# A state-space layer inside a trunk kernel: decay by two heads, exponent on ScalarE, skip and far parts added early

## The chip, the cores and the metric

The kernel runs on one core of a Trainium2 chip. A core has five engines that each run their own instructions in order and wait for one another by semaphores: TensorE (PE: matrix products and transposes; PEld is its weight load), VectorE (DVE), ScalarE (ACT), GpSimd (POOL) and SyncE (SP), which here only issues DMA transfers. Data lies in SBUF; TensorE writes into PSUM. The metric is the time of one execution on the device in microseconds. Before the change it is 2331.98 us, the median of 3 runs (2331.76 to 2332.18).

## What is computed

Two layers with 256 tokens of width 2048: layer 0 mixes tokens by attention (MLA), layer 1 by a Mamba-2 state-space mixer, and each is followed by an MLP with squared ReLU (2048 to 8192 to 2048). The change touches the state-space mixer and, by the size of a DMA ring, the two MLPs. The mixer, cut to what matters (64 heads of 64 in 8 groups, state 128, one chunk of 256 tokens, so the state starts at zero and the second term of y is zero):

```python
zxbcdt = h @ w_in
z, xbc, dt = split(zxbcdt)
xbc = silu(causal_depthwise_conv(xbc, conv_w, conv_b))
xs, b_in, c_in = split(xbc)                    # xs: 8 groups x 8 heads x 64
dt = softplus(dt + dt_bias)
a = -exp(a_log)
# ssd_chunked_scan
x_c = xs * dt
cum = cumsum(dt * a)
decay = exp(where(tril, cum[l] - cum[s], -inf))
cb = einsum('blgn,bsgn->blsg', c, b)
y = einsum('blsgh,bsghp->blghp', cb[..., None] * decay, x_c)
# after the scan
y = y + d_skip * xs
y = y * silu(z)
y = y * rsqrt(mean(y * y over the group's 512) + 1e-6)
return (y * norm_g) @ w_out
```

## The kernel before

**Products in three parts.** Every weight piece (128 x 1024, float32, `wraw`, loaded by SyncE at L88) is split into a high half `wh`, rounded by ScalarE (L103), and a low half `wl`, the rest, by VectorE (L104). A product of float32 is then three products: high by high (L324), low of the activations by high of the weights (L325), high by low of the weights (L328). The MLPs use the same with a scheme of seven products (L595 to L597), in which some weight pieces are summed by VectorE and some by a GpSimd DMA that adds into SBUF as it lands (L200, `wrx`). A flow object loads six pieces ahead and converts three ahead.

**Order.** TensorE runs in the order in which the program is written. The order of the other engines is set by the tile scheduler from its own estimates, and buffers come from pools of fixed numbers.

**Stages.** Attention runs from 0 to about 262 us of the profiled execution, the first MLP to about 945, the state-space mixer from about 960 to 1668, the second MLP to 2330.

**The state-space mixer runs by ticks.** A block of weight products is a list of keys; one key is 24 matmuls, after which `tick()` runs what `later(n, fn)` has put off by n ticks, and then `pump()`. `SSM_ORDER` names the blocks: x0 to x7 (the x of a group, with its convolution), z0 to z7 (its gate), and o0 to o3 (the output projection). A `z` block of group g is named two steps or so after its `x`, so while x of group g + 2 is brought in, the gate of group g is finished.

- *x of a group* (`x_block`, L1159 on): after the convolution TensorE transposes x into PSUM (L1173), ScalarE copies it to SBUF as two halves `xtm` (L1175), GpSimd multiplies the first half by `edge` (L1183), and one tick later TensorE forms the part of the second 128 tokens that comes from the first 128 (`far`, L1187), which VectorE scales into `far` (L1189).
- *a head* (L1203 on): SyncE broadcasts one row of `cumD`, the cumulated log decay, to 128 partitions (`cm`, L1207). VectorE adds the negative of the own row's value and takes the minimum with 0 (L1211, twice), ScalarE takes the exponent (L1212), VectorE multiplies by dt and by the scores `cb` (L1214, twice). A tick later TensorE multiplies by x (L1223).
- *the end of a group*, in the eighth head's product: GpSimd multiplies x by the skip gain `dg` (L1227, twice) and adds `far` to the second half (L1229), VectorE adds half of that to y from PSUM (L1230, twice).
- *the gate* (`z_block`): GpSimd multiplies by the gate (L1255, twice), ScalarE sums squares (L295), then VectorE L288, GpSimd L289 (a power of −0.5), VectorE L1259 and L1261 (twice), and one tick later TensorE transposes the result (L309) for the output projection, which ScalarE and VectorE evacuate as two halves (L298, L299).

Small helpers that record instructions for many callers have one line each: L103, L104, L288, L289, L295, L309, L376 (gain tiles), L419 (the residual sum).

## Time and profile before

| what | value |
|---|---|
| median of the runs | 2331.98 us |
| the profiled execution | 2332.54 us, span 2330.6 us |
| TensorE busy | 2313.0 us, 99% of the span, granted clock 1.00 |
| VectorE busy | 1907.8 us, 82% |
| ScalarE busy | 1384.4 us, 59% |
| GpSimd busy | 193.2 us, 8% |
| DMA | 510.74 MB, mean 219 GB/s |

A line number is a line of the kernel, and a row of a group or of the timeline reads: line, engine, operation, the tile written, an arrow, the tiles read, the shape, the number of instructions; then busy time and the mean of one, or in the timeline first the start and the duration. Text in square brackets or behind a bar is idle time of that engine just before, and the instruction that ended it. A timeline row with x2 or x8 is a run of that many equal instructions.

### The profile page before, as it was taken

What the parts mean: (1) busy time and instruction counts of PE and PEld (TensorE: products, weight loads), DVE (VectorE), ACT (ScalarE), POOL (GpSimd) and SP (SyncE); (2) the same over time, 40 slices, a digit from 0 to 9 for tenths busy, and PEclk for the clock granted to TensorE, in tenths of its full rate; (3) what the DMA queues carried; (4) which work ended last, traced back from release to release, by engine and by line L of the source; (5) the groups of instructions that cost most, each with busy time, mean ns of one, the idle gap of its engine ahead of it and who ended that gap; (6) DMA issues with size and microseconds to landing.
All of it is one profiled execution on the core that took longest, in us unless ns stands there. A gap on an engine that the chain in (4) does not pass through costs nothing. (4 is left out here: it accounts for less than half of the span.)

```text
span 2330.6 us, 30315 instructions
## 1 busy us (share of the span) xinstructions
PE 2313.0 (99%) x10799; PEld 1924.8 (83%) x10799; DVE 1907.8 (82%) x2469; ACT 1384.4 (59%) x1869; POOL 193.2 (8%) x209
## 2 busy tenths in 40 slices
PE   9999999999999999999999999999999999999999
PEld 7788888888888888888888888888888888888887
DVE  7776697998899897677788768666888899989885
ACT  6665566666566656555555455445566656666663
POOL 1331000000000000000022101110000000000000
PEclk9999999999999999999999999999999999999999
DMA  8434678878877877665566666656687888788874
GB/s 310 142 114 142 195 232 254 242 249 255 263 240 247 265 214 247 203 197 180 170 195 201 204 188 194 198 175 201 206 254 231 254 264 239 250 265 246 249 228 164
DMA packets 152151, 510.74 MB, mean 219 GB/s; under 512 B 17152, under 2 KB 26304, under 8 KB 152000
## 3 DMA queue, kind: packets, MB, share of 16 engines
q1 hardware_dynamic: 143712, 479.37, 62.9%
q0 software_dynamic: 8064, 29.36, 7.7%
q8 instruction: 85, 1.39, 0.2%
q14 instruction: 66, 0.54, 0.1%
q10 hardware_dynamic: 224, 0.07, 0.0%
HBM read 506.58 MB, written 2.16 MB: 218 GB/s over the span
## 5 line engine op out<-in xcount | busy, mean ns | idle before, releaser
L103 ACT ACTIVATE wh<-wraw 128x1024 fp32r<-128x1024 f32 (+2 forms) x818 | 859.8, 1054 | 635.2 <-PE acc L325 287.7
L104 DVE TENSOR_TENSOR wl<-wraw,wh 128x1024 fp32r<-128x1024 f32 (+2 forms) x818 | 991.9, 1224 | 250.2 <-ACT wh L103 239.6
L595 PE MATMUL yp<-wh,k 128*128 128x512 f32 x896 | 349.8, 390 | 0.0
L596 PE MATMUL yp<-wl,k 128*128 128x512 f32 x896 | 348.9, 389 | 0.4 <-DVE wl L104 0.3
L597 PE MATMUL yp<-wh,k 128*128 128x512 f32 x896 | 348.8, 389 | 0.0
L324 PE MATMUL acc<-wh,xt 128*128 128x512 f32 x704 | 280.4, 398 | 2.6 <-ACT wh L103 2.6
L325 PE MATMUL acc<-wh,xt 128*128 128x512 f32 x704 | 274.7, 390 | 0.0
L103 ACT ACTIVATE wh<-wrx 128x1024 fp32r<-128x1024 f32 x168 | 178.0, 1060 | 136.9 <-PE yp L597 105.3
L104 DVE TENSOR_TENSOR wl<-wrx,wh 128x1024 fp32r<-128x1024 f32 x168 | 203.8, 1219 | 37.4 <-ACT wh L103 37.4
L596 PEld LDWEIGHTS yp<-wl,k 128*128 128x128 f32 x896 | 168.2, 188 | 35.8 <-DVE wl L104 1.3
L597 PEld LDWEIGHTS yp<-wh,k 128*128 128x128 f32 x896 | 168.2, 188 | 35.0
L595 PEld LDWEIGHTS yp<-wh,k 128*128 128x128 f32 x896 | 168.2, 188 | 34.6
L324 PE MATMUL acc<-wh,k 128*128 128x512 f32 x496 | 196.8, 397 | 0.0
L325 PE MATMUL acc<-wh,k 128*128 128x512 f32 x496 | 193.3, 390 | 0.0
L328 PE MATMUL acc<-wl,xt 128*128 128x512 f32 x704 | 188.6, 390 | 0.0
L595 PE MATMUL st<-wh,xt 128*128 128x512 f32 x448 | 176.8, 395 | 0.0
L596 PE MATMUL st<-wl,xt 128*128 128x512 f32 x448 | 174.8, 390 | 0.0
L597 PE MATMUL st<-wh,xt 128*128 128x512 f32 x448 | 174.8, 390 | 0.0
L324 PEld LDWEIGHTS acc<-wh,xt 128*128 128x128 f32 x704 | 132.6, 188 | 30.7 <-ACT wh L103 4.6
L328 PEld LDWEIGHTS acc<-wl,xt 128*128 128x128 f32 x704 | 132.2, 188 | 28.2
L325 PEld LDWEIGHTS acc<-wh,xt 128*128 128x128 f32 x704 | 132.5, 188 | 25.8
L200 POOL DMA_DIRECT2D wrx<-mi x56 | 48.9, 874 | 1140.3 <-DVE wl L104 1034.4
(291 smaller groups left out, 3475.7 us busy)
## 6 DMA issues: line engine op xcount, KB each, us to landing
wraw<-mi SPq DMA_DIRECT2D x256, 512.0 KB, 5.2
wraw<-mo SPq DMA_DIRECT2D x256, 512.0 KB, 5.3
wraw<-si SPq DMA_DIRECT2D x160, 512.0 KB, 4.0
wraw<-so SPq DMA_DIRECT2D x64, 512.0 KB, 4.3
wrx<-mi SPq DMA_DIRECT2D x56, 512.0 KB, 5.2
wrx<-mi POOLq DMA_DIRECT2D x56, 512.0 KB, 8.0
wraw<-wo SPq DMA_DIRECT2D x32, 512.0 KB, 3.6
wraw<-ukv SPq DMA_DIRECT2D x16, 512.0 KB, 5.0
```

What stands on the lines that cost most here:

```text
L103: self.last = nc.scalar.activation(h[:, v], raw[:, v], AF.Copy)
L104: nc.vector.tensor_tensor(lo[:, v], raw[:, v], h[:, v].bitcast(F32), ALU.subtract)
L200: nc.gpsimd.dma_start(st["b11"].tile, quarter(d, 1, 0), accum_op=ALU.add)
L324: nc.tensor.matmul(accs[t][:, :n], ah, wh[:, q, :], start=first and kt + q == 0, stop=False)
L325: nc.tensor.matmul(accs[t][:, :n], al, wh[:, q, :], start=False, stop=False)
L328: nc.tensor.matmul(accs[t][:, :n], lhs(kt + q, t)[0], wl[:, q, :], start=False, stop=en and q == nk - 1)
L595: nc.tensor.matmul(b, ah, wh, start=first and q == 0, stop=False)
L596: nc.tensor.matmul(b, ah, wl, start=False, stop=False)
L597: nc.tensor.matmul(b, al, wh, start=False, stop=last and q == 1)
```

## The change

It has these parts, all in the state-space mixer but the last:

1. Heads are worked by two. One broadcast of 512 values brings the cumulated decay of two heads (`cm`, four buffers as before but twice as wide). `cumT` holds the own values with their sign; ScalarE takes max(0, own − other) by an activation with a bias (L1214, four of 128 wide), and the exponent of its negative in one of 512 (L1215). VectorE then does one product of 512 wide by the scores (L1218).
2. dt is taken out of that product: VectorE makes a copy xd = x · dt from SBUF when x has been evacuated (L1180, twice a group), and the products read `xd`.
3. The skip gain is multiplied into x by GpSimd right after the `edge` product (L1187, twice, in place), and `far` is added by GpSimd as soon as it is there (L1194). At the group's end only VectorE's sum with y is left (L1231).
4. A group counts as ready for its gate one tick later.
5. The y banks are allocated by the helper, the backlog at which a head is taken each tick goes from 4 heads to 2 pairs, and below it a pair is taken every other tick.
6. The ring of descriptors for DMAs issued by GpSimd is set to 4096 bytes.

```diff
-            cm = sp.tile([P, S], F32, tag="cm", name=f"cm{h}", bufs=4)
-            nc.sync.dma_start(cm, cumD[h:h + 1].to_broadcast([P, S]))
-            m = sp.tile([P, 256], F32, tag="mt", name=f"mt{h}", bufs=6)
-            for t in range(2):
-                nc.vector.tensor_scalar(half(t), cm[:, t * P:(t + 1) * P], ncum[:, t, h:h + 1], 0.0, ALU.add, ALU.min)
-            nc.scalar.activation(m, m, AF.Exp)
-            for t in range(2):
-                nc.vector.scalar_tensor_tensor(half(t), half(t), dt[:, t, h:h + 1], cb[g][:, 256 * t:256 * t + P],
-                                               ALU.mult, ALU.mult)
+            m = sp.tile([P, 2, 2, P], F32, tag="cm", name=f"cm{h}", bufs=4)
+            nc.sync.dma_start(m.rearrange("p a t n -> p (a t n)"), cumD[h // 2:h // 2 + 1].to_broadcast([P, 2 * S]))
+            for k in range(2):
+                for t in range(2):
+                    nc.scalar.activation(m[:, k, t], m[:, k, t], AF.Relu, bias=cumT[:, t, h + k:h + k + 1], scale=-1.0)
+            nc.scalar.activation(m, m, AF.Exp, scale=-1.0)
+            v = m.rearrange("p a t n -> p a (t n)")
+            scores = cb[g][:, 0:2].rearrange("p t n -> p (t n)").unsqueeze(1).to_broadcast([P, 2, 2 * P])
+            nc.vector.tensor_tensor(v, v, scores, ALU.mult)
...
                     nc.scalar.activation(x, b, AF.Copy)
                     xg[g].append(x)
-                for i in range(8):
-                    hq.append((g, i, dg))
+                    w = sp.tile([P, 512], F32, tag="xd", name=f"xd{g}_{t}", bufs=4)
+                    nc.vector.tensor_tensor(heads_of(w), heads_of(x), spread(dt[:, t]), ALU.mult)
+                    xd[g].append(w)
+                for i in range(0, 8, 2):
+                    hq.append((g, i))
                 xw = self.scratch()
                 nc.gpsimd.tensor_tensor(heads_of(xw), heads_of(xg[g][0]), spread(edge[:, 0]), ALU.mult)
+                for t in range(2):
+                    nc.gpsimd.tensor_tensor(xg[g][t], xg[g][t], dg, ALU.mult)
 
                 def across():
...
-                    far[g] = sp.tile([P, 512], F32, tag="far", name=f"far{g}", bufs=2)
-                    nc.vector.tensor_tensor(heads_of(far[g]), heads_of(b), spread(edge[:, 1]), ALU.mult)
+                    far = self.scratch()
+                    nc.vector.tensor_tensor(heads_of(far), heads_of(b), spread(edge[:, 1]), ALU.mult)
+                    nc.gpsimd.tensor_tensor(xg[g][1], xg[g][1], far, ALU.add)
...
         def pump():
-            for _ in range(2 if len(hq) > HEAD_BACKLOG else 1):
-                if hq:
-                    g, i, dg = hq.pop(0)
-                    head(g, i, dg)
-                    if i == 7:
-                        break
+            turns[0] += 1
+            if hq and (len(hq) > HEAD_BACKLOG or turns[0] % 2):
+                heads(*hq.pop(0))
...
-                if i == 7:
+                if i == 6:
                     for t in range(2):
                         x = xg[g][t]
-                        nc.gpsimd.tensor_tensor(x, x, dg, ALU.mult)
-                        if t:
-                            nc.gpsimd.tensor_tensor(x, x, far[g], ALU.add)
                         nc.vector.scalar_tensor_tensor(x, x, 0.5, y[t], ALU.mult, ALU.add)
-                    ready.add(g)
+                    self.later(0, lambda: ready.add(g))
...
-HEAD_BACKLOG = 4
+HEAD_BACKLOG = 2
...
-    nc = bacc.Bacc("TRN2", target_bir_lowering=False, num_devices=1)
+    nc = bacc.Bacc("TRN2", target_bir_lowering=False, num_devices=1, dynamic_dma_scratch_size=4096)
```

The edits in the source also change the order that the scheduler gives to the engines. Three places follow.

GpSimd where x of group 5 is brought in, before (`xtm5_0` is the first half of group 5's x, `xtm3_0` and the `st` rows belong to the gate of group 3, `xtm4_0` to the gate of group 4; line, operation, tile written, tiles read, shape):

```order
L1255 TENSOR_TENSOR xtm3_0_11162<-s2_899_12348,xtm3_0_11162 128x512
L1255 TENSOR_TENSOR xtm3_1_11169<-s2_900_12351,xtm3_1_11169 128x512
L1183 TENSOR_TENSOR s2_908_12446<-xtm5_0_12435,edge_8774 128x512
L289 TENSOR_TENSOR st_912_12455<-st_911_12454,mhalf_91 128x2
L1255 TENSOR_TENSOR xtm4_0_11651<-s2_931_12821,xtm4_0_11651 128x512
L1255 TENSOR_TENSOR xtm4_1_11658<-s2_932_12824,xtm4_1_11658 128x512
L1227 TENSOR_TENSOR xtm5_0_12435<-xtm5_0_12435,gb_907_12444 128x512
L1227 TENSOR_TENSOR xtm5_1_12442<-xtm5_1_12442,gb_907_12444 128x512
L1229 TENSOR_TENSOR xtm5_1_12442<-xtm5_1_12442,far5_12582 128x512
```

And after the change:

```order
L1256 TENSOR_TENSOR xtm3_0_11089<-s2_914_12208,xtm3_0_11089 128x512
L1256 TENSOR_TENSOR xtm3_1_11098<-s2_915_12211,xtm3_1_11098 128x512
L1185 TENSOR_TENSOR s2_923_12310<-xtm5_0_12297,edge_8774 128x512
L1187 TENSOR_TENSOR xtm5_0_12297<-xtm5_0_12297,gb_920_12290 128x512
L1187 TENSOR_TENSOR xtm5_1_12306<-xtm5_1_12306,gb_920_12290 128x512
L289 TENSOR_TENSOR st_927_12321<-st_926_12320,mhalf_91 128x2
L1194 TENSOR_TENSOR xtm5_1_12306<-xtm5_1_12306,s2_932_12432 128x512
```

The two skip products of group 5 moved from behind two gates to a place ahead of L289, the power that belongs to the gate of group 3.

VectorE where x of group 4 is brought in, before (`mt37` is head 37's decay, `x00` the residual stream, `wl525` a weight piece's low half; the `st` and `s2` rows are the gate of group 2):

```order
L1214 SCALAR_TENSOR_TENSOR mt37_11864<-mt37_11864,dt_8772,cb4_10170 128x128 x2
L419 TENSOR_TENSOR x00_133<-acc_863_11565,x00_133 128x512
L419 TENSOR_TENSOR x10_137<-acc_864_11566,x10_137 128x512
L104 TENSOR_TENSOR wl525_11701<-wraw525_11585,wh525_11700 128x1024
L288 TENSOR_SCALAR st_871_11670<-st_858_11556 128x2
L1259 TENSOR_TENSOR st_873_11674<-st_872_11671,rs0_141 128x2
L1261 SCALAR_TENSOR_TENSOR s2_859_11557<-xtm2_0_10650,st_873_11674,gb_857_11554 128x512
L1261 SCALAR_TENSOR_TENSOR s2_860_11560<-xtm2_1_10657,st_873_11674,gb_857_11554 128x512
```

And after the change:

```order
L1218 TENSOR_TENSOR cm38_11821<-cm38_11821,cb4_10168 128x512
L419 TENSOR_TENSOR x00_133<-acc_875_11454,x00_133 128x512
L419 TENSOR_TENSOR x10_137<-acc_876_11455,x10_137 128x512
L1180 TENSOR_TENSOR xd4_0_11543<-xtm4_0_11541,dt_8772 128x512
L1180 TENSOR_TENSOR xd4_1_11552<-xtm4_1_11550,dt_8772 128x512
L104 TENSOR_TENSOR wl525_11587<-wraw525_11474,wh525_11586 128x1024
L288 TENSOR_SCALAR st_883_11564<-st_870_11445 128x2
L1260 TENSOR_TENSOR st_885_11568<-st_884_11565,rs0_141 128x2
L1262 SCALAR_TENSOR_TENSOR s2_871_11446<-xtm2_0_10615,st_885_11568,gb_869_11443 128x512
L1262 SCALAR_TENSOR_TENSOR s2_872_11449<-xtm2_1_10624,st_885_11568,gb_869_11443 128x512
```

The two x · dt products stand between the residual sums and L104, and with L104 ahead of the gate's L288.

ScalarE where x of group 3 is brought in, before (`mt26` and `mt27` are heads, `wh508` and `wh509` high halves of weight pieces, the two L295 the square sums of the gate of group 1):

```order
L1212 ACTIVATE mt26_11266<-mt26_11266 128x256
L103 ACTIVATE wh508_11141<-wraw508_11075 128x1024
L1212 ACTIVATE mt27_11274<-mt27_11274 128x256
L103 ACTIVATE wh509_11209<-wraw509_11093 128x1024
L1175 ACTIVATE xtm3_0_11162<-sm_833_11157 128x512
L1175 ACTIVATE xtm3_1_11169<-sm_834_11164 128x512
L295 ACTIVATE s2_837_11178,st_826_11064<-xtm1_0_10364,rs0_141 128x512
L295 ACTIVATE s2_838_11181,st_826_11064<-xtm1_1_10371,rs0_141 128x512
```

And after the change:

```order
L103 ACTIVATE wh508_11066<-wraw508_11004 128x1024
L1214 ACTIVATE cm30_11399<-cm30_11399,cumT_8773 128x128 x4
L1215 ACTIVATE cm30_11399<-cm30_11399 128x512
L103 ACTIVATE wh509_11130<-wraw509_11022 128x1024
L1177 ACTIVATE xtm3_0_11089<-sm_843_11084 128x512
L1177 ACTIVATE xtm3_1_11098<-sm_844_11093 128x512
L295 ACTIVATE s2_846_11107,st_835_10993<-xtm1_0_10349,rs0_141 128x512
L295 ACTIVATE s2_847_11110,st_835_10993<-xtm1_1_10358,rs0_141 128x512
```

The pair of heads 30 and 31, four activations and one exponent, stands ahead of a weight piece and of the evacuation of x.

## The prediction

> **What bounds the kernel now.** First the page: the span and the engines' busy time. The profiled execution took 2332.54 us, 0.56 above the median of the runs (2331.98), with a span of 2330.6.

> ```profile
> span 2330.6 us, 30315 instructions
> PE 2313.0 (99%) x10799; PEld 1924.8 (83%) x10799; DVE 1907.8 (82%) x2469; ACT 1384.4 (59%) x1869; POOL 193.2 (8%) x209
> ```

> TensorE sets the time, and the change adds and removes no matmul. So I looked at the stretch it edits, the state-space stage: one window of 480 us (columns: us, then busy us of PE, PEld, DVE, ACT, POOL, granted clock, DMA share, GB/s), and all that TensorE waits for between 1000 and 1600.

> ```profile
> 1120.00:1600.00 480.00, 478.94 (x2311) 398.23 (x2310) 356.21 (x595) 248.88 (x347) 78.67 (x56) 1.00 0.62 192
> PE sm L1065 <- ACT xtm L1175: 0.5, 1, 0.5
> PE sm L309 <- DVE s L1261: 0.3, 2, 0.2
> ```

> TensorE is idle 480.00 − 478.94 = 1.06 us there, at full clock. That is nearly all the change could win: work taken from VectorE or ScalarE is time TensorE does not wait for. What it can lose has no such cap, so the question is which results that TensorE needs come later.

> **Work that moves off the path.** Groups by line and shape, 1000 to 1600 (count | busy us, mean ns | idle before and its releaser):

> ```profile
> L104 DVE TENSOR_TENSOR wl<-wraw,wh 128x1024 fp32r<-128x1024 f32 x196 | 245.4, 1256 | 106.9 <-ACT wh L103 105.7
> L1214 DVE SCALAR_TENSOR_TENSOR mt<-mt,dt,cb 128x128 f32<-128x128 f32 x128 | 39.4, 349 | 2.6 <-ACT mt L1212 2.3
> L1211 DVE TENSOR_SCALAR mt<-cm,ncum 128x128 f32<-128x128 f32 x128 | 37.7, 338 | 0.0
> L1230 DVE SCALAR_TENSOR_TENSOR xtm<-xtm,y 128x512 f32<-128x512 f32 x16 | 10.9, 684 | 19.6 <-POOL xtm L1229 15.0 <-POOL xtm L1227 4.7
> L103 ACT ACTIVATE wh<-wraw 128x1024 fp32r<-128x1024 f32 x195 | 206.5, 1060 | 216.2 <-PE acc L325 175.8 <-issue 21.3 <-DVE mt L1211 6.9
> L1212 ACT ACTIVATE mt<-mt 128x256 f32<-128x256 f32 x64 | 25.4, 410 | 38.8 <-DVE mt L1211 38.6
> L1155 ACT ACTIVATE cb<-sm 128x128 f32<-128x128 f32 x6 | 1.6, 274 | 3.9 <-DVE cb L1154 3.3 <-PE y L1223 0.6
> L1175 ACT ACTIVATE xtm<-sm 128x512 f32<-128x512 f32 x16 | 8.7, 591 | 1.0 <-PE sm L1173 1.0
> L1229 POOL TENSOR_TENSOR xtm<-xtm,far 128x512 f32<-128x512 f32 x8 | 10.3, 1287 | 0.6
> ```

> VectorE loses L1211 and L1214, 77.1 us, and gains 32 products of 512 wide and 16 x·dt: at L1230's 0.684 each, 32.8. ScalarE loses 64 exponents (25.4 − their merger: 32 of 512 wide at L1175's 0.591 = 18.9) and gains 128 Relu at L1155's 0.274 = 35.1: net +28.6 over some 540 us. I cost all this at nothing: ScalarE was busy 248.9 of 480 us, and its main work, L103, stands idle 216.2 us, 175.8 of them because TensorE has not yet freed a buffer, so weights are converted ahead of need. VectorE also stops waiting 15.0 + 4.7 us for GpSimd ahead of L1230. If that cover were gone, TensorE would show waits on L103 or L104 in its rows; there are none of any size now.

> Small gains I do count. TensorE's order has 9 fewer switches from the state-space products back to weight products. Each costs about what the first start after a switch is late:

> ```profile
> 1382.35 0.48 PE L324 MATMUL acc<-wh,xt 128*128 128x512 f32 x1
> 1382.66 0.40 PE L325 MATMUL acc<-wh,xt 128*128 128x512 f32 x1
> 1382.89 0.39 PE L324 MATMUL acc<-wh,xt 128*128 128x512 f32 x1
> ```

> The starts are 0.31 apart, then 0.23: 0.08 each, so 0.7. The two present L309 waits (group 4 below: 0.28 late, and stretched to 1.29 from 1.03; 0.5 each) would be replaced: 1.1. With 0.1 of other short idles: −1.9.

> **What is late next.** GpSimd runs in order. At each of six places, where x of groups 2 to 7 is evacuated, its row used to be L1183 (x·edge), then L289 (the power −0.5 of a gate two groups back). Now both L1187 multiplies (x·skip) stand between them, and they must wait until VectorE's L1180 has read the same x. Behind L289 stand VectorE's L1259/L1260 and L1261/L1262, and behind these TensorE's transposes L309, one key (24 matmuls) after the transposes of x, at the same place in its order as before. Group 5, timeline (start, us):

> ```profile
> 1375.19 1.03 PE L1173 MATMUL sm<-cst,s 128*128 128x128 f32 x8
> 1375.57 1.23 DVE L104 TENSOR_TENSOR wl<-wraw,wh 128x1024 fp32r<-128x1024 f32 x1 [1.49 <-ACT wh L103]
> 1375.83 1.09 ACT L1175 ACTIVATE xtm<-sm 128x512 f32<-128x512 f32 x2 [0.29 <-PE sm L1173]
> 1376.51 1.20 POOL L1183 TENSOR_TENSOR s<-xtm,edge 128x512 f32<-128x512 f32 x1 [6.37 <-ACT xtm L1175]
> 1378.60 0.70 POOL L289 TENSOR_TENSOR st<-st,mhalf 128x2 f32<-128x2 f32 x1 [0.89 <-DVE st L288]
> 1379.53 1.42 DVE L1261 SCALAR_TENSOR_TENSOR s<-xtm,st,gb 128x512 f32<-128x512 f32 x2
> 1381.56 1.03 PE L309 MATMUL sm<-cst,s 128*128 128x128 f32 x8
> ```

> The slack: L289 ended at 1379.30, L309 was due at 1381.56 = L1173's start + 6.37. How long L289 to L309 takes when it binds is in group 4 below: 1284.95 + 0.71 = 1285.66 to 1286.78, 1.12.

> Whether L1180 and the GpSimd rows overlap is not in the trace, since L1180 is new. The nearest rows are two-operand work from SBUF on both engines at once:

> ```profile
> 1235.58 3.52 POOL L1227 TENSOR_TENSOR xtm<-xtm,gb 128x512 f32<-128x512 f32 x2 [3.11 <-PE y L1223]
> 1235.60 2.33 DVE L104 TENSOR_TENSOR wl<-wraw,wh 128x1024 fp32r<-128x1024 f32 x1
> ```

> L104 took 2.33 against 1.23 alone, and two L1227 3.52 against 2 × 1.29: each waited for the other. [...]

> So I take them one after the other. Group 5: L1183 ends 1377.71; two L1180 by 0.68 → 1379.07; two L1187 by 1.29 → 1381.65; L289 0.70 → 1382.35; 1.12 → 1383.47. L309 is 1.9 late. The other bound, free overlap: L1180s ride along, 1377.71 + 2.58 + 0.70 + 1.12 = 1382.11, 0.55 late. Group 7 has the same order: 1.9. Groups 4 and 6 have VectorE's L104 between L1180 and the gate's L288:

> ```profile
> 1280.13 1.03 PE L1173 MATMUL sm<-cst,s 128*128 128x128 f32 x8
> 1280.74 0.42 ACT L1212 ACTIVATE mt<-mt 128x256 f32<-128x256 f32 x1 [2.94 <-DVE mt L1211]
> 1282.01 1.07 ACT L1175 ACTIVATE xtm<-sm 128x512 f32<-128x512 f32 x2
> 1282.66 1.04 POOL L1183 TENSOR_TENSOR s<-xtm,edge 128x512 f32<-128x512 f32 x1 [3.08 <-ACT xtm L1175]
> 1284.95 0.71 POOL L289 TENSOR_TENSOR st<-st,mhalf 128x2 f32<-128x2 f32 x1 [1.24 <-DVE st L288]
> 1286.78 1.29 PE L309 MATMUL sm<-cst,s 128*128 128x128 f32 x8 [0.16 <-DVE s L1261]
> ```

> L309, due at 1280.13 + 6.37 = 1286.50, was 0.28 late here. Now: L1183 ends 1283.70, + 1.36 + 1.23 + 2.58 = 1288.87, + 0.71 + 1.12 = 1290.70: 4.2 late. But x was evacuated late here (1.88 after L1173, against 0.64 in group 5), behind an exponent that waited 2.94 for VectorE; without that delay it is 1.24 less, 3.0. I take 3.4, nearer the early end, because that wait on VectorE goes away. Groups 2 and 3 have products y (L1223) between the two, which moves L309's due time:

> ```profile
> 1175.83 1.04 PE L1173 MATMUL sm<-cst,s 128*128 128x128 f32 x8
> 1183.44 1.04 PE L309 MATMUL sm<-cst,s 128*128 128x128 f32 x8
> 1228.36 1.03 PE L1173 MATMUL sm<-cst,s 128*128 128x128 f32 x8
> 1235.55 1.04 PE L309 MATMUL sm<-cst,s 128*128 128x128 f32 x8
> ```

> In group 3 they move away, so L309 is due 6.4 after L1173 and not 7.2; 1.9 as in group 5, up to 1.0 more if four Relu, an exponent and an L103 stand ahead of the evacuation on ScalarE: 2.3. In group 2 they stay, L309 is due 7.6 to 7.8 after its L1173, 1.2 to 1.4 more than in group 5: 0.5 to 1.3, I take 0.8.

> Sum: 0.8 + 2.3 + 3.4 + 1.9 + 3.4 + 1.9 = 13.7. A late L309 also runs in two stretched halves (1.29 against 1.03): 6 × 0.26 = 1.6. Together 15.3 − 1.9 = **+13.4**. On the profiled execution: 2332.5 + 13.4 = 2345.9; on the median, 2345.4. Nothing later takes this up: the order of TensorE is fixed and it has no other idle time to give back.

> **The DMA ring.** The smaller ring can bear on GpSimd's accumulating transfers in the two MLPs:

> ```profile
> 432.31 0.87 POOL L200 DMA_DIRECT2D wrx<-mi  x1 [14.85 <-DVE wl L104]
> 440.01 0.87 POOL L200 DMA_DIRECT2D wrx<-mi  x1 [6.83 <-DVE wl L104]
> wrx<-mi POOLq DMA_DIRECT2D x56, 512.0 KB, 8.0
> ```

> Issues are mostly 15 us apart and a transfer lands after 8.0, so one is done before the next is issued. Where two are 7.7 apart a second could wait 0.3 for the first. TensorE waits for none of them now. I take nothing; if the issue waited a whole landing each time, the readers would still need it only some 12 us later.

> **Rivals.** *GpSimd stays hidden* (chance 0.13): the free overlap above. Five places by 0.55 (2.8), five second halves (1.3), less 1.9: +2.2, 2334. Against it are the 2.33 and the 3.52. *It does what it says* (0.07): VectorE's relief brings x and the gate forward by more than the two L1187 cost, the −1.9 alone remains: 2330, not slower. For it: groups 4 and 6 evacuate x late today; against it: in group 5 x is evacuated at once already, and L289 had but 1.1 us to spare (1381.56 − 1.12 − 1379.30). It decides only where L1183's end comes 1.5 us (2.58 − 1.1) or more earlier than now, the L1180s overlapping too. *ScalarE or the ring binds* (0.06): the four Relu and the exponent, 4 × 0.274 + 0.591 = 1.7 us in one piece, delay L103 where its lead is short, or the issue of L200 blocks; ten such places by 1 us on top: 2356. It decides from the point where L103's lead under that piece is below 1.7.

> **How the numbers follow.** The waits by L289, as added up, 0.74. Predicted 2345. The terms' own bounds (0.5 to 1.3, 1.9 to 2.9, 3.0 to 4.2 twice, 1.9 or a little below) give +11 to +17, and partial overlap +5 to +11; 2335 to 2351 holds these and leaves out the heavy case and most of the two light ones. A measurement of this kernel tells no change from one below about 0.2%, 4.7 us. Slower by more: 0.78; within: 0.18; faster by more: 0.04, since only 1.06 us of idle is there to be won.

> **What would show it.** Right: TensorE's waits list L309 behind VectorE's L1262 six times, 0.5 to 4 us each, in place of 0.3 in all; on GpSimd, L289 starts right at the end of the second L1187; L1187's durations or L1180's stand above 1.29 and 0.68 where they meet; busy time of VectorE falls by about 44 us and that of ScalarE rises by about 29. Wrong: L1187 running beside L1180 at full speed (the light rival), L309 waiting less than 3 us in all, or waits on L103, L104 or L596 that were not there (the heavy one).

## The result, and the profile after

The changed kernel takes 2358.31 us (median of 4 runs, 2357.40 to 2359.62) against 2331.9 before, a ratio of 1.0111 with a 95% interval of 1.0099 to 1.0124: 26.4 us slower. The prediction named the side and the mechanism's place, but 2345 was half of the loss, and its range ended at 2351.

The page of the changed kernel, span and busy time:

```profile
span 2356.3 us, 30115 instructions
PE 2319.1 (98%) x10799; PEld 1928.8 (82%) x10799; DVE 1889.2 (80%) x2261; ACT 1416.2 (60%) x1965; POOL 193.0 (8%) x209
```

The span is 25.7 longer. TensorE's idle time went from 2330.6 − 2313.0 = 17.6 to 2356.3 − 2319.1 = 37.2, so 19.6 of it is idle time; the other 6.1 is busy time, though it runs the same products. Both have their place. What TensorE waits for after 1000 us:

```profile
PE sm L309 <- DVE s L1262: 18.5, 6, 6.4
PE sm L1064 <- ACT xtm L1177: 1.6, 2, 1.1
PE yp L596 <- DVE wl L104: 0.9, 1, 0.9
```

L309 now waits six times, once at each place that the prediction named: 1.42, 2.26, 5.77, 1.34, 6.40 and 1.34 us for groups 2 to 7. The added busy time is a lower clock right behind three of these waits. Stretches of the wait itself (groups 3 and 5) and of the 6 us behind it, for groups 3, 4, 5 and 6 (stretch, us, then busy us and number of instructions of PE, PEld, DVE, ACT, POOL, granted clock, DMA share, GB/s):

```profile
1236.00:1240.20 4.20, 2.01 (x9) 1.31 (x7) 2.25 (x5) 1.15 (x2) 3.14 (x3) 1.00 0.37 109
1240.20:1246.20 6.00, 5.93 (x23) 4.85 (x24) 4.24 (x6) 2.26 (x3) 0.00 (x0) 0.72 0.74 213
...
1298.70:1304.70 6.00, 5.93 (x24) 5.17 (x25) 4.37 (x6) 2.26 (x3) 0.00 (x0) 0.72 0.89 286
1395.00:1396.30 1.30, 0.01 (x1) 0.04 (x1) 1.06 (x3) 0.14 (x1) 0.17 (x1) 1.00 0.52 172
1396.30:1402.30 6.00, 5.97 (x30) 4.93 (x31) 5.20 (x6) 2.39 (x4) 0.00 (x0) 1.00 0.62 179
...
1453.90:1459.90 6.00, 6.00 (x20) 5.09 (x21) 3.99 (x5) 1.80 (x3) 0.00 (x0) 0.56 0.77 252
```

Behind the waits of 2.26, 5.77 and 6.40 us the granted clock averages 0.72, 0.72 and 0.56 over 6 us; behind those of 1.3 to 1.4 it stays at 1.00. At that clock 0.28 × 6 + 0.28 × 6 + 0.44 × 6 = 6.0 us of work is not done: the added busy time.

Now a short wait, group 5, and a long one, group 4, in the timeline of the changed kernel:

```profile
1388.44 1.03 PE L1175 MATMUL sm<-cst,s 128*128 128x128 f32 x8
1389.08 1.09 ACT L1177 ACTIVATE xtm<-sm 128x512 f32<-128x512 f32 x2 [0.29 <-PE sm L1175]
1389.76 1.20 POOL L1185 TENSOR_TENSOR s<-xtm,edge 128x512 f32<-128x512 f32 x1 [6.38 <-ACT xtm L1177]
1389.97 2.14 DVE L1180 TENSOR_TENSOR xd<-xtm,dt 128x512 f32<-128x512 f32 x2
1391.63 2.87 POOL L1187 TENSOR_TENSOR xtm<-xtm,gb 128x512 f32<-128x512 f32 x2 [0.68 <-POOL s L1185]
1392.02 1.26 DVE L288 TENSOR_SCALAR st<-st 128x2 f32<-128x2 f32 x1
1394.47 0.69 POOL L289 TENSOR_TENSOR st<-st,mhalf 128x2 f32<-128x2 f32 x1
1396.29 1.29 PE L309 MATMUL sm<-cst,s 128*128 128x128 f32 x8 [1.34 <-DVE s L1262]
```

```profile
1282.94 0.42 SPq L1211 DMA_DIRECT2D cm<-cumD  x1
1286.50 1.03 PE L1175 MATMUL sm<-cst,s 128*128 128x128 f32 x8
1287.85 1.28 ACT L1214 ACTIVATE cm<-cm,cumT 128x128 f32<-128x128 f32 x4 [3.73 <-DMA cm<-cumD]
1289.17 0.63 ACT L1215 ACTIVATE cm<-cm 128x512 f32<-128x512 f32 x1
1290.65 1.06 ACT L1177 ACTIVATE xtm<-sm 128x512 f32<-128x512 f32 x2
1293.04 3.80 POOL L1187 TENSOR_TENSOR xtm<-xtm,gb 128x512 f32<-128x512 f32 x2 [0.68 <-POOL s L1185]
1293.43 2.29 DVE L104 TENSOR_TENSOR wl<-wraw,wh 128x1024 fp32r<-128x1024 f32 x1
1295.64 1.22 DVE L288 TENSOR_SCALAR st<-st 128x2 f32<-128x2 f32 x1
1296.94 0.70 POOL L289 TENSOR_TENSOR st<-st,mhalf 128x2 f32<-128x2 f32 x1
1298.77 1.94 PE L309 MATMUL sm<-cst,s 128*128 128x128 f32 x8 [5.77 <-DVE s L1262]
```

In group 5 the sequence is the one foretold: L1185, L1180 alongside but longer (2.14 us for the two, 2 × 0.68 foretold), both L1187, and L289 at their very end. In group 4 it starts late. ScalarE stands for 3.73 us in front of a Relu whose broadcast was issued at 1282.94 and had not landed. The copy of x (L1177) is behind it in ScalarE's order and starts 4.15 us after its transposes; in group 5 that is 0.64. Group 6 repeats it (the Relu waits 4.36, the copy starts 4.78 late).

### The profile page after: what moved, and what is told of

The parts are those of the page before. It is cut to its first block, busy times and chain, and to the rows that moved or that the text cites. A ratio compares the mean times of both kernels' runs of the same rounds, so it can differ in the third digit from the quotient of the medians.

```text
span 2356.3 us, 30115 instructions
## 1 busy us (share of the span) xinstructions
PE 2319.1 (98%) x10799; PEld 1928.8 (82%) x10799; DVE 1889.2 (80%) x2261; ACT 1416.2 (60%) x1965; POOL 193.0 (8%) x209
## 4 chain that ended last, share of the span: by engine, by line
PE 93%; DVE 2%; DMA 1%; ACT 1%; POOL 1%; issue 1%; SPq 0%; DVEq 0%; ACTq 0%; POOLq 0%
PE acc L324 12%; PE acc L325 12%; PE acc L328 11%; PE yp L596 9%; PE yp L597 9%; PE yp L595 9%; PE st L596 7%; PE st L597 7%; PE st L595 7%; PE sm L309 2%; DVE wl L104 1%; PE y L1227 1%; DMA cm<-cumD 1%; ACT wh L103 1%; PE acc L595 1%
## 5 line engine op out<-in xcount | busy, mean ns | idle before, releaser
L103 ACT ACTIVATE wh<-wraw 128x1024 fp32r<-128x1024 f32 (+2 forms) x818 | 858.7, 1053 | 614.7 <-PE acc L325 298.9
L104 DVE TENSOR_TENSOR wl<-wraw,wh 128x1024 fp32r<-128x1024 f32 (+2 forms) x818 | 994.7, 1229 | 277.3 <-ACT wh L103 267.2
L596 PE MATMUL yp<-wl,k 128*128 128x512 f32 x896 | 348.9, 389 | 0.9 <-DVE wl L104 0.9
L595 PE MATMUL yp<-wh,k 128*128 128x512 f32 x896 | 349.8, 390 | 0.0
L324 PE MATMUL acc<-wh,xt 128*128 128x512 f32 x704 | 280.5, 398 | 2.4 <-ACT wh L103 2.3
L325 PE MATMUL acc<-wh,xt 128*128 128x512 f32 x704 | 275.1, 391 | 0.0
L103 ACT ACTIVATE wh<-wrx 128x1024 fp32r<-128x1024 f32 x168 | 177.9, 1059 | 135.5 <-PE yp L597 102.4
L104 DVE TENSOR_TENSOR wl<-wrx,wh 128x1024 fp32r<-128x1024 f32 x168 | 203.8, 1218 | 35.1 <-ACT wh L103 34.9
L596 PEld LDWEIGHTS yp<-wl,k 128*128 128x128 f32 x896 | 168.2, 188 | 36.2 <-DVE wl L104 1.6
L324 PE MATMUL acc<-wh,k 128*128 128x512 f32 x496 | 197.8, 399 | 0.0
L595 PEld LDWEIGHTS yp<-wh,k 128*128 128x128 f32 x896 | 168.2, 188 | 34.8
L325 PE MATMUL acc<-wh,k 128*128 128x512 f32 x496 | 194.6, 392 | 0.0
L595 PE MATMUL st<-wh,xt 128*128 128x512 f32 x448 | 176.8, 395 | 0.0
L596 PE MATMUL st<-wl,xt 128*128 128x512 f32 x448 | 174.8, 390 | 0.0
L324 PEld LDWEIGHTS acc<-wh,xt 128*128 128x128 f32 x704 | 132.8, 189 | 30.8 <-ACT wh L103 4.6
L325 PEld LDWEIGHTS acc<-wh,xt 128*128 128x128 f32 x704 | 132.8, 189 | 26.0
L200 POOL DMA_DIRECT2D wrx<-mi x56 | 49.0, 875 | 1140.7 <-DVE wl L104 1011.4
## 6 DMA issues: line engine op xcount, KB each, us to landing
wraw<-mi SPq DMA_DIRECT2D x256, 512.0 KB, 5.2
wraw<-mo SPq DMA_DIRECT2D x256, 512.0 KB, 5.2
wraw<-si SPq DMA_DIRECT2D x160, 512.0 KB, 4.3
wraw<-so SPq DMA_DIRECT2D x64, 512.0 KB, 4.0
wrx<-mi SPq DMA_DIRECT2D x56, 512.0 KB, 5.0
wrx<-mi POOLq DMA_DIRECT2D x56, 512.0 KB, 8.0
wraw<-wo SPq DMA_DIRECT2D x32, 512.0 KB, 3.6
wraw<-ukv SPq DMA_DIRECT2D x16, 512.0 KB, 4.7
```

The lines of the kernel that those rows point to most:

```text
L103: self.last = nc.scalar.activation(h[:, v], raw[:, v], AF.Copy)
L104: nc.vector.tensor_tensor(lo[:, v], raw[:, v], h[:, v].bitcast(F32), ALU.subtract)
L200: nc.gpsimd.dma_start(st["b11"].tile, quarter(d, 1, 0), accum_op=ALU.add)
L324: nc.tensor.matmul(accs[t][:, :n], ah, wh[:, q, :], start=first and kt + q == 0, stop=False)
L325: nc.tensor.matmul(accs[t][:, :n], al, wh[:, q, :], start=False, stop=False)
L595: nc.tensor.matmul(b, ah, wh, start=first and q == 0, stop=False)
```

## The experiments

The theory to test: the skip products on GpSimd make the gate late (A), and in groups 4 and 6 ScalarE's queue adds to it (A', A''). Where the expectations say "lock", they mean what the kernel before shows where the two engines met: L104 took 2.33 us against 1.23, and two L1227 3.52 against 2 × 1.29. The first four runs each take away one supposed cause, and all three at once.

**1. Skip products behind the gate's power.**

```diff
-                for t in range(2):
-                    nc.gpsimd.tensor_tensor(xg[g][t], xg[g][t], dg, ALU.mult)
...
+                    with self.tc.issue_after(self.power.ins):    # in across(), ahead of far; power is L289
+                        for t in range(2):
+                            nc.gpsimd.tensor_tensor(xg[g][t], xg[g][t], dg, ALU.mult)
```

> The changed kernel with one edit: the two skip products of GpSimd are issued behind L289, the power of the gate two groups back, as before the change, and not ahead of it; all else stays. Theory A (the order on GpSimd costs the waits): the four short waits of TensorE on L309 (1.42, 2.26, 1.34, 1.35 us) go to under 0.5 each; the two long ones (5.77 and 6.40) lose the 1.9 us that the second L1187 outlasts VectorE's L104, and about 4 each stay. L309 waits 8 to 9 us in all and not 18.5, about 2345 us. Rival B (the waits come from the late copy of x on ScalarE and from VectorE's lock, not from the order): the four short waits stay above 1 each, 2354 to 2358.

Measured: 2356.96 us (2355.50 to 2357.88), so rival B's number. L309 waits 16.0 us in all and not 8 to 9; only group 6 gained much (4.49 in place of 6.40). The rows say why, and it is neither theory (group 5, the gate's scaling is L1261 and L1263 here):

```profile
1392.64 0.70 POOL L289 TENSOR_TENSOR st<-st,mhalf 128x2 f32<-128x2 f32 x1 [1.31 <-DVE st L288]
1393.31 2.53 POOL L1194 TENSOR_TENSOR xtm<-xtm,gb 128x512 f32<-128x512 f32 x2
1393.38 1.24 DVE L1261 TENSOR_TENSOR st<-st,rs 128x2 f32<-128x2 f32 x1 [0.82 <-POOL st L289]
1394.66 2.40 DVE L1263 SCALAR_TENSOR_TENSOR s<-xtm,st,gb 128x512 f32<-128x512 f32 x2
1396.54 1.29 PE L309 MATMUL sm<-cst,s 128*128 128x128 f32 x8 [1.19 <-DVE s L1263]
```

L289 starts 3.81 us after x's transposes (1388.83) and not 6.03, as wanted. Then the skip products run at once behind it, and VectorE's next two steps meet them: a 128x2 product of 0.16 us takes 1.24, the two scalings 2.40 in place of 1.41. What L289 won is given back one step later: L309 starts 7.71 after the transposes, and 7.85 in the changed kernel. So the order on GpSimd alone is not the cause: here the products cost behind L289 nearly what they cost ahead of it.

**2. Six buffers for the decay.**

```diff
-            m = sp.tile([P, 2, 2, P], F32, tag="cm", name=f"cm{h}", bufs=4)
+            m = sp.tile([P, 2, 2, P], F32, tag="cm", name=f"cm{h}", bufs=6)
```

> The changed kernel with six instead of four buffers for the decay of two heads (cm), all else the same. Theory A' (at groups 4 and 6 ScalarE stands behind a Relu that waits for its broadcast, which is issued late because the buffer is held until TensorE's product has read it): ScalarE's waits on the DMA of cm (3.7 and 4.4 us there) vanish, the copy of x starts 0.7 us after its transposes and not 4.2 to 4.8, the two long waits fall from 5.8 and 6.4 to 2 to 3 each, and the slow clock behind them goes: about 2348 us. Rival C (the broadcast is late for the queue of SyncE, not for the buffer): no change, 2357 to 2359.

Measured: 2356.38 us (2353.96 to 2358.07), where about 2348 was expected. The long waits shrank to 4.16 and 4.63, not to 2 to 3, because the Relu still waits for its broadcast. The issue of the broadcast comes right behind that of a weight piece (L88), which had waited for VectorE:

```profile
SPq L88 <- DVE wl L104: 4.3, 1, 4.3
1282.53 0.33 SPq L88 DMA_DIRECT2D wraw<-so  x1
1282.91 0.42 SPq L1211 DMA_DIRECT2D cm<-cumD  x1
1287.38 1.28 ACT L1214 ACTIVATE cm<-cm,cumT 128x128 f32<-128x128 f32 x4 [2.10 <-DMA cm<-cumD]
1287.65 1.03 PE L1175 MATMUL sm<-cst,s 128*128 128x128 f32 x8
1290.17 1.07 ACT L1177 ACTIVATE xtm<-sm 128x512 f32<-128x512 f32 x2
```

The broadcast is issued when it was in the changed kernel (1282.91 against 1282.94), and there too it stands behind an L88 (1282.56) that waited 4.3 us for L104. So at this place rival C holds: SyncE's queue comes last and not the buffer, which in the changed kernel was free 1.8 us before the issue, when TensorE's product ended at 1281.12. The Relu waits 2.10 and not 3.73, and the copy of x starts 2.5 late and not 4.15, mostly because TensorE's transposes come 1.15 us later in this run. With more buffers the scheduler also brings in a later pair at that place (the 22nd broadcast, not the 20th), so the Relu in front of the copy is again one whose data is on its way.

**3. x times dt from PSUM.**

```diff
-                    nc.vector.tensor_tensor(heads_of(w), heads_of(x), spread(dt[:, t]), ALU.mult)
+                    nc.vector.tensor_tensor(heads_of(w), heads_of(b), spread(dt[:, t]), ALU.mult)
```

> The changed kernel with x times dt read by VectorE from the transposes in PSUM and not from ScalarE's copy in SBUF; all else the same. Theory A (VectorE's products with two inputs in SBUF and GpSimd's hold each other up): L1180 takes 0.7 each without waiting, L1187 starts when L1185 ends, L289 is about 1 us earlier, so that the short waits fall from 1.3 to 0.3 and all six by about 1: 2350 to 2352 us. Rival D (no lock, the products merely queue up on GpSimd): L1187 stays where it is and the time within 1.5 us of 2358.

Measured: 2354.50 us (2353.82 to 2357.55). The short waits of groups 5 and 7 fall from 1.34 to 0.30, as theory A has it (group 5):

```profile
1389.29 1.20 POOL L1185 TENSOR_TENSOR s<-xtm,edge 128x512 f32<-128x512 f32 x1 [6.37 <-ACT xtm L1177]
1389.50 1.28 DVE L1180 TENSOR_TENSOR xd<-sm,dt 128x512 f32<-128x512 f32 x2
1390.45 2.54 POOL L1187 TENSOR_TENSOR xtm<-xtm,gb 128x512 f32<-128x512 f32 x2
1394.78 1.29 PE L309 MATMUL sm<-cst,s 128*128 128x128 f32 x8 [0.30 <-ACT wh L103]
```

(The last row names L103, but L309 starts 0.89 us behind the start of L1262 here as in the changed kernel, so the gate still releases it.) Reading PSUM, the two L1180 take 1.28 beside L1185, against 2.14 when both inputs were in SBUF, and L1187 starts as soon as L1185 ends, against 0.68 us behind it. So here the two engines held each other up more while L1180 read both inputs from SBUF. Part of the gain is lost elsewhere: L1180 now reads the PSUM bank too, and TensorE waits 4.9 us for it at groups 0 and 1 (L1064), against 1.6 for the copy of x in the changed kernel.

**4. All three edits.**

> The changed kernel with all three edits: skip products behind L289, six buffers for cm, x times dt from PSUM. Theory A and A' together: no wait of TensorE on L309 above 0.3, no slow clock, 2330 to 2333 us, at most 2 under the kernel before, since that had 1.06 us of idle in this stage. Rival E (something else of the change costs time too, the gates one step later or the work on ScalarE): 2336 or more.

Measured: 2359.40 us (2358.89 to 2360.30), no better than the changed kernel. L309 still waits 14.5 us in five places (2.00 in group 3, 0.82 in groups 5 and 7, 5.4 and 5.5 in groups 4 and 6), and L1064 5.3 us. This is rival E's number, but the rows show the causes that were there already: in group 4 the Relu, ahead of the copy, still waits 3.01 us for its broadcast; in group 5 the two scalings take 2.41 beside the skip products; and L1064 has the wait of experiment 3. Whether another part of the change costs time too, this run can't say; experiment 8 does. These causes called for two better edits: the skip products out of the gate altogether, and ScalarE's heads behind the copy.

**5. The wait filled with idle transposes.** TensorE runs 36 transposes of a constant ahead of the gate's own in groups 2 and 4 (their x-places are groups 4 and 6); the result is overwritten.

```diff
+        for _ in range(fill):        # 36 for g in (2, 4) and t == 0, else 0
+            self.nc.tensor.transpose(b[:, 0:P], self.ident, self.ident)
```

> The changed kernel with 36 idle transposes of TensorE (about 4.7 us) written ahead of the gate's own in groups 2 and 4, where it stood idle for 5.77 and 6.40 us; their result is overwritten. Theory F (a wait of more than some 2 us is followed by about 5 us at a lower granted clock, which costs 2 us or more each time): the clock behind these two waits stays at 1.0 and not 0.5 to 0.66, the L309 rows start at the same time as without the fill, and the time falls by 3 to 5 us, 2353 to 2355. Rival G (the low clock is not the cause, or comes from the load of the moment): no change or slower.

Measured: 2353.16 us (2350.52 to 2356.30), 5.1 under the changed kernel although in group 4 nothing that the gate waits for came sooner: its transposes start 12.19 us behind those of x, and 12.27 in the changed kernel (in group 6, 12.27 and 12.90). TensorE still stands idle for 1.74 and 1.84 us behind the fill. The clock behind it (same columns as above), here for group 3, where the wait is 2.82, and group 4:

```profile
1241.40:1247.40 6.00, 5.89 (x30) 4.87 (x31) 5.28 (x6) 2.29 (x4) 0.00 (x0) 1.00 0.58 201
1298.30:1304.30 6.00, 5.84 (x29) 4.82 (x30) 5.37 (x7) 2.26 (x3) 0.00 (x0) 1.00 0.84 270
```

Both are at 1.00, and group 6 too, so theory F is confirmed for the long waits: with most of the idle time filled the clock stayed at 1.00 where it had averaged 0.72 and 0.56 over 6 us, which had cost 0.28 × 6 = 1.7 and 0.44 × 6 = 2.6 us on top of the waits. The 5.1 us can't be divided exactly: group 6 also came 0.6 sooner, and group 3, which was not filled, kept its clock here after 2.82 us and lost it after 2.26 in the changed kernel. So a wait of this length may or may not be followed by a low clock; the last section shows in what the two differ.

**6. Skip and far at the group's end.** Part 3 of the change undone; the result goes over `xd` once the products have read it.

```diff
+                        nc.gpsimd.tensor_tensor(w, x, dg, ALU.mult)          # w is xd, in product(), i == 6
+                        if t:
+                            nc.gpsimd.tensor_tensor(w, w, far[g], ALU.add)
-                        nc.vector.scalar_tensor_tensor(x, x, 0.5, y[t], ALU.mult, ALU.add)
+                        nc.vector.scalar_tensor_tensor(x, w, 0.5, y[t], ALU.mult, ALU.add)
```

> The changed kernel with part 3 undone: GpSimd multiplies x by the skip gain and adds far only at the group's end, where the products have read xd (the result is written over xd), as before the change. Theory A2 (the skip products cost whenever they fall between the copy of x and the end of L262's scaling of the gate, ahead of L289 by the order and behind it by keeping VectorE out of SBUF): the four short waits of L309 vanish (under 0.4), the two long ones shrink to about 4 each; 8 to 9 us of L309 waits in all, about 2342. Rival H (VectorE's L1180 alone makes the gate late): short waits of 0.5 to 1 stay.

(L262 there is a slip for L1262; "keeping VectorE out of SBUF" rests on experiment 1, where beside the skip products L1261 took 1.24 us and not 0.16, and two L1263 2.40 and not 1.41.) Measured: 2344.60 us (2343.58 to 2345.74), 13.7 under the changed kernel. All waits of L309:

```profile
PE sm L309 <- DVE s L1262: 6.0, 4, 2.6
```

They are 0.29, 0.94, 2.17 and 2.56, in groups 2, 3, 4 and 6; those of groups 5 and 7 are gone, and the 0.94 of group 3 is more than was expected of a short one. The long waits are shorter than the 4 each that were expected: in group 4 the Relu now waits 2.27 for its broadcast and not 3.73, and the copy of x starts 2.70 after its transposes and not 4.15. Behind these two waits the clock still averages 0.72 over 6 us.

**7. ScalarE's heads behind the copy of x.**

```diff
+            with self.tc.issue_after(self.copied.ins):      # copied: the latest L1177
                 for k in range(2):
                     for t in range(2):
                         nc.scalar.activation(m[:, k, t], m[:, k, t], AF.Relu, ...)
                 nc.scalar.activation(m, m, AF.Exp, scale=-1.0)
```

> The changed kernel with one edit: ScalarE's Relu and exponent of a pair of heads are issued behind the copies of x that stand ahead of them in the program, and not ahead of these. Theory A'' (in groups 4 and 6 ScalarE waits 3.7 and 4.4 us for a pair's broadcast with the copy of x queued behind): the copy starts 0.7 us after its transposes there, the two long waits fall to 2 to 3 us, the short ones stay; L309 waits 11 to 12 us in all, about 2349 us. Rival I (the copy is not what binds, GpSimd and VectorE are): the long waits stay above 4.

Measured: 2344.09 us (2341.78 to 2345.96), 14.2 under the changed kernel, more than expected. In group 4 the copy of x starts 0.63 us behind its transposes. The long waits fell to 2.23 each, three short ones stayed (1.37, 1.35, 1.35), and group 2's wait went too. No stretch behind a wait has a lower clock, which is part of the gain and in part luck: waits of 2.17 and 2.26 elsewhere were followed by one. Group 4:

```profile
1287.40:1289.60 2.20, 0.02 (x1) 0.00 (x0) 1.34 (x4) 1.39 (x3) 1.02 (x2) 1.00 0.34 76
1289.60:1295.60 6.00, 5.91 (x30) 4.87 (x31) 6.00 (x8) 4.78 (x11) 0.00 (x0) 1.00 0.89 276
```

**8. Both.** The edits of 6 and 7 together.

> Skip and far at the group's end, and ScalarE's heads behind the copy of x, together. Theory A2 with A'': no wait on L309 above 0.5 and no low clock; 2331 to 2334 us, so level with the kernel before. Rival H (L1180 or ScalarE's added work costs on its own): 2336 or more.

Measured: 2333.20 us (10 runs, 2331.98 to 2335.06), a ratio to the kernel before of 1.0003 with an interval of 0.9994 to 1.0013: the whole loss is gone, and nothing is won that can be told from noise. Page and waits of TensorE after 1000 us:

```profile
span 2329.8 us, 30119 instructions
PE 2314.0 (99%) x10799; PEld 1925.9 (83%) x10799; DVE 1874.9 (80%) x2261; ACT 1415.2 (61%) x1965; POOL 193.2 (8%) x209
PE sm L1064 <- ACT xtm L1177: 1.0, 2, 0.5
```

VectorE has 32.9 us less to do than before the change and ScalarE 30.8 more, and the time is the same: before the change TensorE waited for the two only 1.0 us between 1000 and 1600.

**9. The ring alone.** The kernel before, with the ring of 4096 bytes as its only edit.

```diff
-    nc = bacc.Bacc("TRN2", target_bir_lowering=False, num_devices=1)
+    nc = bacc.Bacc("TRN2", target_bir_lowering=False, num_devices=1, dynamic_dma_scratch_size=4096)
```

> The kernel before the change with the 4096-byte ring for GpSimd's DMAs as its only edit. My theory (a transfer is done before the next is issued): L200 takes 0.87 us as before, nothing waits for it, 2331 to 2333 us. Rival (the ring makes issues wait): L200's rows grow where two stand 7.7 us apart, waits of TensorE on L596 or L595 appear in the two MLPs, 2334 or more.

Measured: 2332.81 us (11 runs, 2331.81 to 2334.14), ratio 1.0003, interval 0.9994 to 1.0012. L200 takes 48.9 us in all for 56, as before. The ring costs nothing that can be seen.

## Why the prediction was half right, by its own steps

**What bounds the kernel, and the ceiling on a gain: right.** Experiment 8 has the pairs of heads and their relief for VectorE, but neither the early skip products nor the waits on L309, and it stands level with the kernel before. The 1.9 us of small gains that were counted can't be told from nothing in it; its profile has one stretch of low clock in attention (0.51 from 80.56 to 84.03, up to 1.7 us) that the profile of the kernel before has not, so they aren't excluded either.

**Work at no cost: right for the work itself, with VectorE's share mis-sized.** ScalarE's busy time rose by 31.8 us (28.6 foretold). VectorE's fell by 18.6 and not 44. L1180 took 15.7 in place of 11, and L288 6.4 more in all than before (8.8 against 2.4 for 14), in the rows where GpSimd's products ran beside them (2.14 for two L1180, 1.26 for one L288 in group 5). The 44 also adds single durations that overlap in part (two L1211 of 0.28, the median, span 0.48), so that even experiment 8, where L288 is as short as before but L1180 still takes 15.9, shows 32.9. The weight halves kept their lead: no wait of TensorE on L103 or L104 grew by more than 0.6. What did cost was not the added work on ScalarE but its place in the order, as follows.

**The short waits: right in mechanism, and in sum partly by luck.** Groups 2, 3, 5 and 7 were put at 0.8, 2.3, 1.9 and 1.9, 6.9 in all, and measured 1.42, 2.26, 1.34 and 1.34, 6.4 in all. That the two engines make each other wait was taken from L1227 (3.52 for two) and L104 (2.33), and experiment 3 shows it for L1180 itself (2.14 for two beside L1185, 1.28 when it read PSUM). The estimate for groups 5 and 7 was high by 0.6: the L1180 begin beside L1185, so that the first L1187 starts 3.19 us behind the transposes and not 3.88. Group 2 was low by 0.6: there, too, x is copied late (2.08 us) behind a Relu that had waited for its broadcast.

**The long waits: mis-sized, 3.4 each against 5.77 and 6.40.** The step that failed is "I take 3.4, nearer the early end, because that wait on VectorE goes away". The late copy of x before the change was laid to an exponent that waited for VectorE; that wait went, but in its place came a Relu that waits for a DMA, 3.73 and 4.36 us, with the copy behind it. The prediction had the row that priced the old wait and did not ask what ScalarE's new first step waits for. Before the change no engine waited for a broadcast between 1000 and 1600: in group 4 the one that L1211 read at 1280.23 had been issued at 1254.3, and the delay came from VectorE's own queue, where an L1230 ahead waited 1.96 us for GpSimd. After it, the broadcast read at 1287.85 had been issued only at 1282.94; ScalarE waits for broadcasts 26 times, 43.7 us in all, and in groups 4 and 6 the copy of x stands behind such a wait. Putting the copy first (experiment 7) brings these waits of L309 to 2.23. The two terms are 12.2 − 6.8 = 5.4 us of the miss.

**The lower clock: not in the sum at all, 6.0 us.** The working priced each wait at its own length (and 0.26 for the second half of the transposes). Experiment 5 shows that the clock behind a long wait is a price of its own (1.00 behind the filled waits, against 0.72 and 0.56 over 6 us), and the prediction put it at nothing without a reason.

These two make 11.4 of the 12.3 us between +13.4 and the measured +25.7 of the profiled execution. L1064 adds 1.1, since it waits 1.6 and not 0.5, again for a copy of x, and the short waits take 0.5 off; the last 0.3 is not accounted for.

**The rivals.** *GpSimd stays hidden* is excluded by the six waits. *It does what it says* is excluded, and experiment 8, the nearest to it that ran, gives 2333 and not 2330. *ScalarE or the ring binds* was nearest in its number (2356), yet neither by the ring (experiment 9) nor by L103: ScalarE bound through the order of its steps.

## What to carry to other kernels

Where the bottleneck engine is 99% busy, as here, relief of other engines has next to nothing to win (in experiment 8 VectorE had 32.9 us less to do, at a ratio of 1.0003), and the question for each moved step is what stands behind it in its engine's queue. Price that from the row that the queue's first instruction waits for after the change, a DMA's landing above all, not from the wait that the change removes. In this kernel a wait of TensorE of 2 us or more could cost its length and 1.7 to 2.6 us more, by a lower clock behind it (0.72 to 0.56 over 6 us). And a GpSimd product delayed VectorE's steps with two SBUF inputs (two L1180 took 2.14 us beside L1185), and L288 (1.26 and not 0.16), where they met, so it belongs where no short chain is running, not merely behind the urgent instruction.

## What the runs showed of the hardware

**A single small VectorE instruction took about as long as a GpSimd product beside it.** L288 has 128x2 values and one tile as input; it takes 0.15 to 0.17 alone, and 1.26 and 1.22 where a L1187 runs (two L1187 take 2.87 and 3.80 there). I had expected this of instructions with two inputs in SBUF only, as L104 has them in the rows of the prediction. Why L288 is held up too, no run shows.

```profile
1237.27:1240.68 3.41, 1.16 (x8) 0.70 (x6) 1.47 (x3) 0.94 (x1) 1.87 (x2) 1.00 0.30 74
1240.68:1244.09 3.41, 3.41 (x12) 2.71 (x11) 3.41 (x5) 1.20 (x2) 0.00 (x0) 0.50 0.61 124
1244.09:1247.50 3.41, 3.41 (x17) 2.78 (x16) 1.39 (x2) 1.06 (x1) 0.00 (x0) 1.00 0.74 270
...
1285.35:1288.76 3.41, 2.07 (x10) 1.37 (x8) 2.55 (x4) 3.41 (x7) 3.07 (x3) 1.00 0.05 4
1288.76:1292.17 3.41, 2.48 (x15) 2.05 (x16) 3.41 (x5) 1.82 (x5) 0.00 (x0) 1.00 0.93 288
```

The first wait lies in one window, of which TensorE is idle for 2.25 us, and the next window runs at half the clock. The second is divided, with 1.34 and 0.93 us of idle time in its two windows, and no low clock follows. In all eight kernels with such waits (the changed one and experiments 1 to 7), a window at full clock in which L309 waited 1.97 us or more was followed by a low one, and a window in which it waited 1.86 or less was not; of three waits of L1064 that put 1.77 to 1.81 us into one window (experiments 3 and 4) one was followed by a low one, so the bound is not exact, and no run shows what sets it. Experiment 7 was lucky in this, as both of its waits of 2.23 were divided.
